# Set steps for the loads of states and decay sums, and a state-space visit spread over three steps, in a one-core decoder layer

## The chip, the cores and the metric

The kernel runs on one core of one Trainium2 chip. The metric is the device time of one execution in microseconds (us). The kernel before has a median of 1779.08 us over three runs (1777.47 to 1779.08).

## The reference

One inference step of a decoder layer for 256 prompt tokens and 64 sample tokens (8 sequences of 8), 320 tokens together, in fp32. One input projection makes the columns of two head groups; a gated MLP and a state-space mixer (SSD) work on them; an output projection adds both up; a convolutional FFN follows.

```python
x = x + RMSNorm_post( W_out [ chunkMLP(h) || SSD(h) ] ),   h = RMSNorm_pre(x)
x = x + RMSNorm_post( ConvFFN(RMSNorm_pre(x)) )
# SSD, per head:
h_t = exp(dt_t a) h_{t-1} + dt_t x_t B_t^T,  y_t = h_t C_t
```

The SSD has 32 heads in 4 groups of 8. The prompt is computed in two chunks of 128 tokens as products with decay matrices. The 8 sample sequences each start from a stored state (64 x 128 per head) that the kernel must read, decay, add to and write back: per group 8 loads and 8 stores of 128 x 512 values.

## The kernel before

**Products.** Each fp32 weight is split into a rounded high part and the remainder, each activation likewise, and three matmuls give one fp32 product (`accumulate`, lines 151 to 156). Weights come in slabs of 512 KB (`slab`, line 110): SyncE loads `wraw` (three buffers), ScalarE casts it to `whi` (line 124), VectorE subtracts to get `wlo` (line 125); both also have three buffers. A slab is 24 matmuls of 128 x 128 by 320. `project` (line 189) runs 8 slabs into four PSUM banks of the pool `mm`, one per 128 columns, and hands each bank to an eviction function; `chunk_out` (line 248) multiplies 512 rows of the output weight in 16 column blocks through the same four banks and adds each block into an accumulator on VectorE (line 261). A second pool, `ms`, has four banks for everything else.

**Order of the work.** SyncE, ScalarE and VectorE take their instructions in the order in which a scheduler puts them when the program is built. Inside the state-space part the stages come in a row by hand (lines 1121 to 1137): X1 (the x columns of group 1), chunk 3, z0 (the z columns of group 0, `heads_out`), X2, chunk 4, z1, X3, chunk 5, z2, z3, chunk 6, chunk 7, and then the FFN. The X projections evict through `conv_proj` (lines 467 to 480): two multiplies into `pad`, one ScalarE and three VectorE steps of the convolution `cv` (line 474), then SiLU. The z projections evict through `scaled` (line 405).

The state-space work of a group runs between these matmuls. `ssd(g)` (line 855) is a generator; a list `bg` holds the generators, and `tick` (line 175) is called after each slab (line 211) and after two column blocks of a chunk. It runs the next step of the first generator once as many matmuls have been issued as that step asked for at its last `yield`; `advance` (line 166) keeps these due counts. Each group has these steps:

- visit 0 (lines 861 to 934): loads six state tiles `st` (three pairs; `load_state`, line 868) and the fourth pair into two buffers of the tag `cs`; copies x of the samples fourfold (`x4`); transposes x; makes `cb` and `cms`. It ends with `yield 120 if g == 0 else 48`.
- the big visit (lines 936 to 998): transposes of the samples' x (`x_of_samples`), the prompt's first chunk state `s1`, the products of C with all four state pairs (`with_c`, line 948), for group 0 the casts of b (`b_of_samples`, lines 837 to 842, which read `b4`), both splits of x (`samples_split`, lines 901 to 908: `xq`, `xsp` and the multiplies into `xdt`), the multiplies of `yo_to_xdt` (line 978), and the decay of the fourth pair on GpSimd (`shrunk`, line 959).
- 13 steps (lines 1046 to 1064): `end(i)` adds the new part to a state pair and stores it from ScalarE's queue; `shrunk` decays a pair; `decays` (line 1006) makes decay factors for a head, and for every second head loads the sums it needs (`load_sums`, line 875) into a `cs` buffer at that moment and exponentiates a part of them (`cpx`, line 1012); `products(j)` (line 1025) multiplies for two heads.
- `final`, which adds and stores the prompt's state.

The z projections are called with `quiet=4`: no step runs after their last slabs. At the end of a z projection, `z_evac` runs any steps still missing.

Of the kernel before, what the change touches and what calls it, by code (L numbers as in the profile page):

```python
# [9 lines left out]
F32 = mybir.dt.float32  # L10
# [3 lines left out]
ALU = mybir.AluOpType  # L14
# [20 lines left out]
def hybrid_step(  # L35
# [115 lines left out]
    def accumulate(ps, w, xhi, xlo, first, last):  # L151
        whi, wlo = w
        made_so_far[0] += 3
        pe.matmul(ps, whi, xhi, start=first, stop=False)  # L154
        pe.matmul(ps, whi, xlo, start=False, stop=False)  # L155
        return pe.matmul(ps, wlo, xhi, start=False, stop=last).ins  # L156

# [5 lines left out]

    bg, side, due, made_so_far = [], [], {}, [0]

    def advance(tasks, task):

        try:
            due[task] = made_so_far[0] + (next(task) or 0)
            return True  # L170
        except StopIteration:
            tasks.remove(task)
            return False

    def tick():
        for task in list(side):
            if made_so_far[0] >= due.get(task, 0):
                advance(side, task)
        while bg and made_so_far[0] >= due.get(bg[0], 0):
            if advance(bg, bg[0]):  # L180
                return
# [7 lines left out]
    def project(w, c0, evac, width=512, spare=False, late=None, quiet=0, ready=None, after=None, ahead=1, rate=1, more=None, held=None):  # L189
# [248 lines left out]
    def in_order(ap):  # L438

        return ap.rearrange("p (i j f) -> p j i f", j=4, f=32)  # L440
# [6 lines left out]
    with ExitStack() as mctx:  # L447
# [374 lines left out]
        with tc.tile_pool(name="sd", bufs=1) as sd:  # L822
# [7 lines left out]
            for c in range(2):  # L830
                act.copy(btok[:, c].rearrange("p (j i f) -> p j i f", j=4, f=32), in_order(b_raw[:, 512 * c:512 * c + 512]))
            b4 = sd.tile([P, 2, 512], F32, tag="xsp", name="b4", bufs=1)
            for i in range(2):
                o = NP + 32 * i
                sp.dma_start(b4[:, i], b_d[o:o + 32].unsqueeze(0).broadcast_to([4, 32, 512]))

            def b_of_samples():
                for i in range(2):
                    act.copy(bsp[:, i].rearrange("p (j i f) -> p j i f", j=4, f=32), in_order(b4[:, i]))
                    for rs in (slice(32, 64), slice(96, P)):  # L840
                        h = bsp[rs, i].rearrange("p (j i f) -> p j i f", j=4, f=32)
                        dve.tensor_tensor(out=h, in0=in_order(b4[rs, i]), in1=h.bitcast(F32), op=ALU.subtract)

# [11 lines left out]
            def ssd(g):  # L855
# [4 lines left out]

                def load_state(i):

                    if i < 3:
                        st = [sd.tile([P, 512], F32, tag="st", name="st", bufs=6) for _ in range(2)]
                    else:
                        st = [sd.tile([P, 2, NT], F32, tag="cs", name="st3", bufs=3).rearrange("p i n -> p (i n)")[:, :512] for _ in range(2)]
                    for h in range(2):
                        sp.dma_start(st[h], state_ssm[4 * h + i, g])
                    return st

                def load_sums(j):
# [23 lines left out]
                def x_of_samples(i):  # L895
                    ps = misc("xt_ps")
                    for j in range(4):
                        by_token(ps[:, P * j:P * j + P], rows[i][:, P * j:P * j + P], 0)
                    return ps

                def samples_split(i, ps):
                    xq = sd.tile([P, 512], F32, tag="xde", name="xq", bufs=2)
                    times(xq, ps, 3 + i)
                    act.copy(xsp[:, i], xq)
                    dve.tensor_tensor(out=xsp[64:, i], in0=xq[64:], in1=xsp[64:, i].bitcast(F32), op=ALU.subtract)
                    for r in range(2):
                        at = slice(64 - 64 * r + 32 * i, 96 - 64 * r + 32 * i)
                        times(xdt[at, 2, 256 * r:256 * r + 256], ps[at, 256 * r:256 * r + 256], 2, at, slice(4 * r, 4 * r + 4))

                for c in range(2):  # L910
# [4 lines left out]
                    if c == 0:  # L915
                        x0d = decayed(0, 0)
                rows.append(fourfold(sd.tile([P, 4, P], F32, tag="xde", name="x4", bufs=2), xs, 1).rearrange("p k n -> p (k n)"))
                ps = misc("cb_ps")
# [20 lines left out]
                s1 = sd.tile([P, 512], F32, tag="s1", name="s1", bufs=1)  # L939

                ps_yo = misc("yo_ps")

                def with_c(i, st):

                    for r in range(2):
                        for h in range(2):
                            row = 64 * r + 32 * h
                            pe.matmul(ps_yo[row:row + 32, :256], cms[:, 4 * h + i, :], st[h][:, 256 * r:256 * r + 256],
                                      start=i == 0, stop=i == 3, tile_position=(0, row))

# [37 lines left out]
                for i in range(4):  # L988
                    with_c(i, sts[i])
# [35 lines left out]
                def products(j):  # L1025
# [9 lines left out]
                    def hs(hl):  # L1035
# [9 lines left out]
                                             op0=ALU.mult, op1=ALU.add)  # L1045
                ends = {2: 3, 4: 0, 6: 1, 9: 2}
                heads = {0: 0, 1: 1, 3: 2, 4: 3, 5: 4, 7: 5, 8: 6, 10: 7}
                for n in range(13):
                    if n == 0:
                        for i in (3, 0):  # L1050
                            bms[i] = picked(i)
                    if n in ends and not (n == 9 and g == 3):
                        end(ends[n])
                    if n in (2, 4):
                        bms[n // 2] = picked(n // 2)
                    if n in (1, 3, 5):
                        shrunk(n // 2, sts[n // 2])
                    if n in heads:
                        decays(heads[n])
                    if n in (7, 12):  # L1060
                        products(0 if n == 7 else 2)
                        products(1 if n == 7 else 3)
                    if n < 12:
                        yield 24

# [11 lines left out]
                if g == 3:  # L1077
                    rest.extend([lambda: end(2, pool), final()])
                else:
                    yield 24  # L1080
                    for _ in final():
                        pass
# [4 lines left out]
            def heads_out(g):  # L1087
# [4 lines left out]
                def z_evac(j, ps):  # L1092
# [3 lines left out]
                    with first():  # L1096
                        scaled(ps, AF.Silu, zs)
                        dve.tensor_tensor(out=y[:, j, :], in0=y[:, j, :], in1=zs, op=ALU.mult)
                        add_square(ssq, y[:, j, :], j == 0, dve)
                project(w_in, Z0 + 512 * g, z_evac, quiet=4)  # L1100

                def norm():
                    yield 24
                    small = partial_sums(ssq, ssq_d[g])
                    yield 24
                    rb = tp.tile([P, NT], F32, tag="pv", name="rb", bufs=4)
# [369 lines left out]
```

## Time and profile before

| | |
|---|---|
| median of 3 runs | 1779.08 us |
| profiled execution | 1780.13 us |
| its span (first to last instruction) | 1778.3 us |
| granted TensorE clock, mean | 0.998 |
| TensorE busy | 1762.1 us (99%) |
| VectorE busy | 1179.3 us (66%) |
| ScalarE busy | 827.1 us (47%) |
| GpSimd busy | 288.6 us (16%) |
| HBM read and written | 274.21 MB, 15.50 MB |

The profile comes from one execution of the program. PE is TensorE, PEld its weight loads, DVE VectorE, ACT ScalarE, POOL GpSimd, SP SyncE. L125 is line 125 of the kernel. Busy time is that of instructions that compute or copy; what an engine waited for is inferred from semaphore events, and the name behind an arrow is the one that came last. The clock is what the throttle granted to TensorE, 1.00 being full speed.

### The profile page before, as it was taken

Reading aid. Unit: us, or ns where it says so; the run is one execution under the profiler, and the core shown is the slowest. Engines: PE = TensorE matmul, PEld = TensorE weight load, DVE = VectorE, ACT = ScalarE, POOL = GpSimd, SP = SyncE. Lnnn points to the kernel's source line nnn. Section 1 sums busy time; section 2 is a strip of 40 time slices with the busy share of each in tenths; the row PEclk is TensorE's granted clock in tenths of the full one; section 3 lists DMA queues with packets and bytes.
Section 4 is the critical chain, followed back from the end, with each engine's and each line's share of the span. In section 5 each row is a group of like instructions: output and inputs, shape, how many; then the busy total and the mean of one; then the engine's idle time right before and its main releaser. Section 6 shows DMA issues by size and latency. Waiting matters only on the chain.

```text
span 1778.3 us, 30601 instructions
## 1 busy us (share of the span) xinstructions
PE 1762.1 (99%) x11881; PEld 1713.0 (96%) x11881; DVE 1179.3 (66%) x2020; ACT 827.1 (47%) x1199; POOL 288.6 (16%) x624
## 2 busy tenths in 40 slices
PE   9999999999999999999999999999999999999998
PEld 7789999999999989999999999999999999999998
DVE  7549764656868688887865475656656565656575
ACT  5434554333555656655645334343434343433445
POOL 1202220000303131303121011110102010101004
PEclk9999999999999999999999999999999999999999
DMA  7556654555574757655554455454454544554542
GB/s 258 162 151 174 192 169 149 155 154 148 176 237 137 241 163 225 191 156 169 167 159 154 149 152 155 146 157 147 152 154 149 151 152 149 157 151 148 155 150 103
DMA packets 218362, 291.73 MB, mean 164 GB/s; under 512 B 19624, under 2 KB 146984, under 8 KB 218024
## 3 DMA queue, kind: packets, MB, share of 16 engines
q1 hardware_dynamic: 205688, 269.37, 50.2%
q10 hardware_dynamic: 10016, 14.16, 2.2%
q0 software_dynamic: 2512, 6.23, 1.2%
q8 instruction: 94, 1.54, 0.4%
q14 instruction: 52, 0.43, 0.1%
HBM read 274.21 MB, written 15.50 MB: 163 GB/s over the span
## 4 chain that ended last, share of the span: by engine, by line
PE 90%; DVE 5%; DMA 3%; ACT 1%; issue 1%; SPq 0%; ACTq 0%; DVEq 0%
PE ps L154 18%; PE ps L156 18%; PE ps L155 18%; PE pd L155 9%; PE pd L156 9%; PE pd L154 9%; PE ps_v L144 7%; DVE wlo L125 2%; DMA cs<-dacs_d 1%; DMA out_ssm_state_sample<-st 1%; ACT whi L124 1%; PE y_ps L1033 1%; DMA st<-in_state_ssm 0%; PE sg L780 0%; DMA small<-ssq_d 0%
## 5 line engine op out<-in xcount | busy, mean ns | idle before, releaser
L125 DVE TENSOR_TENSOR wlo<-wraw,whi 128x1024 fp32r<-128x1024 f32 (+1 forms) x476 | 582.6, 1225 | 429.8 <-ACT whi L124 427.6
L124 ACT CAST whi<-wraw 128x1024 fp32r<-128x1024 f32 (+1 forms) x475 | 494.7, 1042 | 691.7 <-PE ps L155 363.1
L154 PE MATMUL ps<-h_hi,whi 128*128 128x320 f32 x2268 | 704.2, 311 | 4.5 <-ACT whi L124 2.3
L156 PE MATMUL ps<-h_hi,wlo 128*128 128x320 f32 x2268 | 701.9, 310 | 2.0 <-DVE wlo L125 2.0
L155 PE MATMUL ps<-h_lo,whi 128*128 128x320 f32 x2268 | 701.9, 310 | 0.0
L154 PEld LDWEIGHTS ps<-h_hi,whi 128*128 128x128 f32 x2268 | 426.1, 188 | 8.4 <-ACT whi L124 2.8
L156 PEld LDWEIGHTS ps<-h_hi,wlo 128*128 128x128 f32 x2268 | 426.0, 188 | 2.9 <-DVE wlo L125 2.8
L155 PEld LDWEIGHTS ps<-h_lo,whi 128*128 128x128 f32 x2268 | 426.3, 188 | 0.4
L156 PE MATMUL pd<-fhi,wlo 128*128 128x320 f32 x704 | 218.2, 310 | 0.0
L154 PE MATMUL pd<-fhi,whi 128*128 128x320 f32 x704 | 218.2, 310 | 0.0
L155 PE MATMUL pd<-flo,whi 128*128 128x320 f32 x704 | 218.2, 310 | 0.0
L154 PE MATMUL pd<-ohi,whi 128*128 128x320 f32 x448 | 138.6, 309 | 0.1
L156 PE MATMUL pd<-ohi,wlo 128*128 128x320 f32 x448 | 138.2, 309 | 0.0
L155 PE MATMUL pd<-olo,whi 128*128 128x320 f32 x448 | 138.1, 308 | 0.0
L154 PEld LDWEIGHTS pd<-fhi,whi 128*128 128x128 f32 x704 | 132.1, 188 | 0.0
L155 PEld LDWEIGHTS pd<-flo,whi 128*128 128x128 f32 x704 | 132.1, 188 | 0.0
L156 PEld LDWEIGHTS pd<-fhi,wlo 128*128 128x128 f32 x704 | 132.1, 188 | 0.0
L1241 POOL COPY ptf<-pad 128x2 f32<-128x2 f32 x88 | 21.2, 240 | 602.7 <-DVE pad L1229 602.0
L261 DVE TENSOR_TENSOR acc_ffn<-acc_ffn,pd 128x320 f32<-128x320 f32 (+1 forms) x161 | 77.5, 482 | 37.8 <-PE pd L156 36.3
L154 PEld LDWEIGHTS pd<-ohi,whi 128*128 128x128 f32 x448 | 84.1, 188 | 1.3 <-issue 0.9
L155 PEld LDWEIGHTS pd<-olo,whi 128*128 128x128 f32 x448 | 84.1, 188 | 0.3
L156 PEld LDWEIGHTS pd<-ohi,wlo 128*128 128x128 f32 x448 | 84.1, 188 | 0.1
(333 smaller groups left out, 1890.0 us busy)
## 6 DMA issues: line engine op xcount, KB each, us to landing
wraw<-in_ffn_w_up SPq DMA_DIRECT2D x176, 512.0 KB, 3.7
wraw<-in_w_in SPq DMA_DIRECT2D x140, 512.0 KB, 3.8
wraw<-in_ffn_w_down SPq DMA_DIRECT2D x88, 512.0 KB, 3.4
wraw<-in_w_out SPq DMA_DIRECT2D x64, 512.0 KB, 3.5
st<-in_state_ssm SPq DMA_DIRECT2D x32, 256.0 KB, 4.4
out_ssm_state_sample<-st ACTq DMA_DIRECT2D x30, 256.0 KB, 3.6
cs<-dacs_d SPq DMA_DIRECT2D x16, 320.0 KB, 4.8
xr<-in_xT SPq DMA_DIRECT2D x4, 640.0 KB, 4.5
```

Of the source, the lines that this page charges most:

```text
L124: rounded[:] = [act.copy(hi, raw).ins]
L125: dve.tensor_tensor(out=lo, in0=raw, in1=hi.bitcast(F32), op=ALU.subtract)
L144: made = pe.matmul(out, xi, w[g][wi], start=first and begins, stop=last and ends)
L154: pe.matmul(ps, whi, xhi, start=first, stop=False)
L155: pe.matmul(ps, whi, xlo, start=False, stop=False)
L156: return pe.matmul(ps, wlo, xhi, start=False, stop=last).ins
L261: added_last[:] = [dve.tensor_tensor(out=acc[:, nb, ts], in0=acc[:, nb, ts], in1=ps[:, ts], op=ALU.add).ins]
L1033: pe.matmul(ps[64 * i:64 * i + 64, cols], w(hl), x(hl, m, cpx), tile_position=(0, 64 * i), **flags)
L1241: pool.tensor_copy(ptf[:, k, :], pad[:, 256:258])
```

## The change

The generators now yield two numbers: the matmuls until the next step is due, and the least room it wants. `tick` is told how many matmuls the projection still has for its open banks, and runs a step only if that is enough; a chunk always has room (10000). The z projections lose `quiet=4`. A variable `last_made` keeps the last matmul of `accumulate`, so that loads can be put behind it in the order (`tc.issue_after`; this orders the program and adds no semaphore of TensorE to the loads).

For each group:

- state pairs of the next group are loaded at steps 7, 9 and 12 of this one (group 0's are loaded in its visit 0); the fourth pair is loaded into `cs` buffers (`st3`) in visit 0 for the products with C alone, and loaded again into `st` buffers at step 4, to be decayed, added to and stored;
- sums are loaded in visit 0 (pair 0), at step 0 (pairs 1 and 2) and at step 7, or 6 for the last group (pair 3);
- the big visit stops after the first split of x; the second split is step 0, the multiplies into `xdt` and `yo_to_xdt` are step 1. Group 0's big visit is due after 96 matmuls and not 120, which puts it behind the fifth of X1's eight slabs in the built order, and not into chunk 3; group 1's visit 0 goes from behind z0 to two slabs before z0's end;
- group 0's copies of b are loaded after the fourth pair and the first sums, into buffers of `s1` and `xde` and not that of `xsp`, and `b_of_samples` is ordered behind the last product with C;
- state ends run in the order 0, 1, 2, 3 (before 3, 0, 1, 2), and the last group has one step less.

Cut to its core:

```diff
-    def tick():
+    def tick(room=10000):
+        def may(task):
+            at, least = due.get(task, (0, 0))
+            return made_so_far[0] >= at and room >= least
...
-                    tick()
+                    tick(3 * nb * (KD - k0 - nk) if nb == len(js) else 24 if js[0] == 0 else 0)
...
-            b4 = sd.tile([P, 2, 512], F32, tag="xsp", name="b4", bufs=1)
-            for i in range(2):
-                o = NP + 32 * i
-                sp.dma_start(b4[:, i], b_d[o:o + 32].unsqueeze(0).broadcast_to([4, 32, 512]))
+            b4 = [sd.tile([P, 512], F32, tag=tag, name="b4", bufs=n) for tag, n in (("s1", 1), ("xde", 2))]
...
-                sts = [load_state(i) for i in range(3)]
-                rows = [sd.tile([P, 2, NT], F32, tag="cs", name="x4", bufs=3).rearrange("p i n -> p (i n)")[:, :512]]
-                fourfold(rows[0].rearrange("p (k n) -> p k n", n=P), xs, 0)
-                sts.append(load_state(3))
+                sts = sts_of[g]
+                if g == 0:
+                    sts += [load_state(0, i) for i in range(3)]
+                st3 = [sd.tile([P, 2, NT], F32, tag="cs", name="st3", bufs=3).rearrange("p i n -> p (i n)")[:, :512] for _ in range(2)]
+                for h in range(2):
+                    sp.dma_start(st3[h], state_ssm[4 * h + 3, g])
+                cs_of = {0: load_sums(0)}
+                if g == 0:
+                    for i in range(2):
+                        o = NP + 32 * i
+                        sp.dma_start(b4[i], b_d[o:o + 32].unsqueeze(0).broadcast_to([4, 32, 512]))
...
-                yield 120 if g == 0 else 48
+                yield 96 if g == 0 else 48, 72
...
                 if g == 0:
-                    b_of_samples()
+                    with tc.issue_after(visited):
+                        b_of_samples()
...
-                for i in range(2):
-                    samples_split(i, ps_x[i])
+                samples_split(0, ps_x[0])
                 act.copy(s1, ps_s)
-                yo_to_xdt()
-                shrunk(3, sts[3])
-                yield 24
+                yield 24, 0
...
-                        cs = load_sums(j)
+                        cs = cs_of[j]
...
-                ends = {2: 3, 4: 0, 6: 1, 9: 2}
-                heads = {0: 0, 1: 1, 3: 2, 4: 3, 5: 4, 7: 5, 8: 6, 10: 7}
-                for n in range(13):
+                ends = {2: 0, 5: 1, 7: 2, 10: 3}
+                picks = {0: (0, 1), 2: (2,), 5: (3,)}
+                shrinks = {0: 0, 3: 1, 5: 2, 8: 3}
+                e = 1 if g == 3 else 0
+                heads = {0: 0, 1: 1, 3: 2, 4: 3, 5: 4, 7: 5, 9 - e: 6, 10 - e: 7}
+                states = {4: (g, 3), 7: (g + 1, 0), 9: (g + 1, 1), 12: (g + 1, 2)}
+                decays_of = {0: (1, 2), 7 - e: (3,)}
+                for n in range(13 - e):
...
+                        samples_split(1, ps_x[1])
+                    if n == 1:
+                        for i in range(2):
+                            samples_rows(i, ps_x[i])
+                        yo_to_xdt()
...
+                    with tc.issue_after(last_made[0]):
+                        for j in decays_of.get(n, ()):
+                            cs_of[j] = load_sums(j)
+                        if n in states and states[n][0] < 4:
+                            sts_of[states[n][0]].append(load_state(*states[n]))
...
-                    if n < 12:
-                        yield 24
+                    if n < 12 - e:
+                        yield 24, 48 if n + 1 in (0, 1, 2, 5, 7, 10) and (g < 3 or n < 7) else 0
...
-                project(w_in, Z0 + 512 * g, z_evac, quiet=4)
+                project(w_in, Z0 + 512 * g, z_evac)
```

More of the change, by code (lines that the diff above doesn't have):

```diff
@@ L1 @@
 from contextlib import ExitStack, contextmanager, nullcontext
-from itertools import repeat
 import concourse.bass as bass
@@ L155, in accumulate @@
         pe.matmul(ps, whi, xlo, start=False, stop=False)
-        return pe.matmul(ps, wlo, xhi, start=False, stop=last).ins
+        last_made[0] = pe.matmul(ps, wlo, xhi, start=False, stop=last).ins
+        return last_made[0]
     def rows_of(w, k0, nk, c0, n):
@@ L831, in hybrid_step, with load_state @@
                 act.copy(btok[:, c].rearrange("p (j i f) -> p j i f", j=4, f=32), in_order(b_raw[:, 512 * c:512 * c + 512]))
-            b4 = sd.tile([P, 2, 512], F32, tag="xsp", name="b4", bufs=1)
-            for i in range(2):
-                o = NP + 32 * i
-                sp.dma_start(b4[:, i], b_d[o:o + 32].unsqueeze(0).broadcast_to([4, 32, 512]))
+            b4 = [sd.tile([P, 512], F32, tag=tag, name="b4", bufs=n) for tag, n in (("s1", 1), ("xde", 2))]
             def b_of_samples():
                 for i in range(2):
-                    act.copy(bsp[:, i].rearrange("p (j i f) -> p j i f", j=4, f=32), in_order(b4[:, i]))
+                    act.copy(bsp[:, i].rearrange("p (j i f) -> p j i f", j=4, f=32), in_order(b4[i]))
                     for rs in (slice(32, 64), slice(96, P)):
                         h = bsp[rs, i].rearrange("p (j i f) -> p j i f", j=4, f=32)
-                        dve.tensor_tensor(out=h, in0=in_order(b4[rs, i]), in1=h.bitcast(F32), op=ALU.subtract)
+                        dve.tensor_tensor(out=h, in0=in_order(b4[i][rs]), in1=h.bitcast(F32), op=ALU.subtract)
+            def load_state(g, i):
+                st = [sd.tile([P, 512], F32, tag="st", name="st", bufs=6) for _ in range(2)]
+                for h in range(2):
+                    sp.dma_start(st[h], state_ssm[4 * h + i, g])
+                return st
+            sts_of = {g: [] for g in range(4)}
             def by_head(ap):
@@ L897, in x_of_samples @@
                     for j in range(4):
-                        by_token(ps[:, P * j:P * j + P], rows[i][:, P * j:P * j + P], 0)
+                        by_token(ps[:, P * j:P * j + P], x4[:, i, P * j:P * j + P], 0)
                     return ps
@@ new lines, in ssd @@
+                picks = {0: (0, 1), 2: (2,), 5: (3,)}
[5 more added lines that the diff above has]
+                for n in range(13 - e):
+                    if n == 0:
+                        samples_split(1, ps_x[1])
+                    if n == 1:
+                        for i in range(2):
+                            samples_rows(i, ps_x[i])
+                        yo_to_xdt()
+                    if n in ends and not (n == 10 and g == 3):
+                        end(ends[n])
+                    for i in picks.get(n, ()):
+                        bms[i] = picked(i)
+                    if n in (6, 12 - e):
+                        products(0 if n == 6 else 2)
+                        products(1 if n == 6 else 3)
+                    with tc.issue_after(last_made[0]):
[3 more added lines that the diff above has]
+                            sts_of[states[n][0]].append(load_state(*states[n]))
+                    if n in shrinks:
+                        shrunk(shrinks[n], sts[shrinks[n]])
@@ L1077, in ssd @@
                 if g == 3:
-                    rest.extend([lambda: end(2, pool), final()])
+                    rest.extend([lambda: end(3, pool), final()])
                 else:
-                    yield 24
+                    yield 24, 24
                     for _ in final():
```

45 lines of the change are left out of this document (16 added, 29 removed).

## The prediction

> **What bounds the kernel now.** I read the page's first part, then the busy time by stretches of time, then the waits of each engine in the stretch that the change touches, and last the chain of waits around each stall.
>
> ```profile
> span 1778.3 us, 30601 instructions
> PE 1762.1 (99%) x11881; PEld 1713.0 (96%) x11881; DVE 1179.3 (66%) x2020; ACT 827.1 (47%) x1199; POOL 288.6 (16%) x624
> ```
> ```profile
> 420.00:835.00 415.00, 405.39 (x2925) 386.97 (x2924) 325.16 (x567) 235.79 (x413) 102.48 (x116) 1.00 0.60 185
> ```
>
> TensorE bounds the kernel: 1778.3 - 1762.1 = 16.2 us of idle time in all. The second fence is one row of the table by stretches (start:end, length, busy PE, PEld, DVE, ACT, POOL, granted clock, DMA share, GB/s). From 420 to 835 us the four groups' state-space work runs between projections, and 415.00 - 405.39 = 9.61 of the 16.2 us are lost there. The diff touches nothing outside, and TensorE does the same products after it: only this idle time, and clock lost with it, can be won. Where it lies:
>
> ```profile
> 438.00:448.00 10.00, 7.47 (x40) 6.94 (x40) 5.05 (x5) 4.36 (x6) 0.00 (x0) 0.83 0.67 191
> 474.00:479.00 5.00, 4.58 (x29) 3.99 (x28) 4.88 (x8) 4.97 (x10) 4.36 (x7) 1.00 0.33 105
> 508.00:514.00 6.00, 4.83 (x32) 4.31 (x31) 2.68 (x5) 4.94 (x12) 0.74 (x1) 1.00 0.44 144
> 554.00:559.00 5.00, 4.38 (x30) 4.12 (x30) 4.90 (x14) 0.38 (x1) 1.03 (x1) 1.00 0.16 46
> 586.00:594.00 8.00, 6.52 (x59) 5.69 (x58) 7.15 (x12) 6.68 (x15) 0.92 (x1) 1.00 0.78 272
> 634.00:642.00 8.00, 5.92 (x39) 5.39 (x38) 8.00 (x11) 5.18 (x11) 4.69 (x4) 1.00 0.13 26
> sum 42.00, PE 33.70 PEld 30.44 DVE 32.65 ACT 26.50 POOL 11.74; mean PE 5.62 PEld 5.07 DVE 5.44 ACT 4.42 POOL 1.96
> ```
> ```profile
> PE ps L154 <- ACT whi L124: 2.3, 2, 1.8
> PE ps L154 <- DVE ev L405: 2.1, 2, 1.2
> PE ps L156 <- DVE wlo L125: 2.0, 3, 0.7
> PE y_ps L1033 <- DVE cs L1022: 1.5, 2, 1.0
> ```
>
> Six stretches of 42.00 us hold 42.00 - 33.70 = 8.30 us of idle time, nearly all of the 9.61. The waits (total, times, longest) say on what: weight halves cast or subtracted late, PSUM banks emptied late, decays late. In the first stretch the clock was also granted at 0.83, so (1 - 0.83) x 10.00 = 1.7 us more went in slower matmuls. So **10.0 us** can be won at most.
>
> The Trainium skill ("TensorE: Matmul & The Clock Gate", Part 1: The HAM clock gate) puts half speed behind an idle window of about 3.4 us. The trace fell to 0.83 with 10.00 - 7.47 = 2.53 us idle. By the page alone the 1.7 us would not be there and the sum below would be 1.7 us less gain; the trace decides.
>
> **The change, part by part.**
>
> *First visit, b's copies.* These are SyncE's, ScalarE's and TensorE's rows (start, duration, idle before):
>
> ```profile
> 429.17 1.25 SPq L835 DMA_DIRECT2D b<-b_d  x2
> 431.28 3.64 SPq L868 DMA_DIRECT2D st<-in_state_ssm  x5
> 443.99 0.38 SPq L118 DMA_DIRECT2D wraw<-in_w_in  x1
> ```
> ```profile
> 435.88 0.62 ACT L839 CAST bsp<-b 128x512 fp32r<-128x512 f32 x1 [4.03 <-DMA b<-b_d]
> 441.14 0.62 ACT L839 CAST bsp<-b 128x512 fp32r<-128x512 f32 x1 [4.12 <-DMA b<-b_d]
> 441.66 1.99 ACT L124 CAST whi<-wraw 128x1024 fp32r<-128x1024 f32 x2
> ```
> ```profile
> 459.13 0.31 PE L156 MATMUL ps<-h_hi,wlo 128*128 128x320 f32 x1
> 462.80 1.03 PE L427 MATMUL xt_ps<-ident,x 128*128 128x128 f32 x8
> 464.63 1.93 PE L948 MATMUL yo_ps<-st,cb_cms 128*32 128x256 f32 x32
> ```
>
> ScalarE takes its instructions in order. The casts of b stood ahead of two weight casts and waited for loads issued at 429 that landed at 435.9 and 441.1; TensorE starved. After the change the copies of b are loaded behind the fourth state pair and cast behind the big visit's state products and one weight slab later. That takes away 2.53 + 1.7 = **4.2 us**.
>
> It also brings work forward. The big visit (transposes, s1, products of C with four state pairs: 462.80 to 464.63 + 1.93, 3.8 us on TensorE) leaves the chunk and goes behind the fifth of X1's eight slabs. Moved, it costs TensorE nothing in itself. A slab is 24 matmuls that start 0.147 us apart, 3.5 us. X1 ended at 459.4, so now at 459.4 - 4.2 + 3.8 = 459.0; three slabs and 3.8 us earlier, at 444.7, the big visit starts. On VectorE, in the built order, these now stand ahead of X1's evictions (the means, ns, are second behind the bar):
>
> ```profile
> L842 DVE TENSOR_TENSOR bsp<-b,bsp 32x512 fp32r<-32x512 f32 x4 | 2.7, 685 | 6.8 <-ACT bsp L839 6.8
> L886 DVE TENSOR_TENSOR xq<-xt_ps,dt 128x512 f32<-128x512 f32 x8 | 5.5, 683 | 0.1
> L1022 DVE TENSOR_TENSOR cs<-cs,cb_cms 128x320 f32<-128x320 f32 x32 | 18.0, 579 | 2.9 <-ACT cs L1020 2.8
> L905 DVE TENSOR_TENSOR xsp<-xq,xsp 64x512 fp32r<-64x512 f32 x8 | 9.2, 1160 | 0.3 <-ACT xsp L904 0.2
> L886 DVE TENSOR_TENSOR xdt<-xt_ps,dt 32x256 f32<-32x256 f32 x16 | 6.7, 420 | 0.4
> L125 DVE TENSOR_TENSOR wlo<-wraw,whi 128x1024 fp32r<-128x1024 f32 x97 | 122.8, 1268 | 39.8 <-ACT whi L124 39.5
> L467 DVE TENSOR_TENSOR pad<-ps,r 128x256 f32<-128x256 f32 x12 | 5.0, 414 | 0.0
> L468 DVE TENSOR_TENSOR pad<-ps,r 128x64 f32<-128x64 f32 x12 | 2.5, 210 | 0.0
> L474 DVE SCALAR_TENSOR_TENSOR cv<-pad,prm,cv 128x344 f32<-128x344 f32 x36 | 22.6, 654 | 1.1 <-ACT cv L472 1.1
> ```
>
> Let the second copy of b land at t. Its cast ends at t + 0.6 (the 0.62 above), two of the four bsp subtracts at t + 2.0, two xq 3.4, one cs 3.9; the xsp subtracts wait for ScalarE's casts of them and end at about 7.5 (an estimate), two xdt 8.3, wlo 9.6, the first bank's two pads 10.2. From there follow two xdt, one yo multiply (taken as 0.42 like xdt), pads, one cv, wlo, pads, three cv, wlo and the fourth bank's pads: 0.84 + 0.42 + 0.62 + 0.65 + 1.27 + 0.62 + 1.96 + 1.27 + 0.62 = 8.3, so t + 18.5. The pool has four banks, so chunk 3's first column block (12 matmuls, 1.76 us) needs bank 0 at 459.0 and its fourth needs bank 3 at 459.0 + 5.3 = 464.3. So nothing is lost while t is below 464.3 - 18.5 = **445.8**, and each us beyond costs one.
>
> When is t? A slab is cast once TensorE has left the slab three before, and its raw buffer is loaded again after its subtract. X1's sixth slab is cast from 444.7 - 7.0 = 437.7, subtracted by 440.0; the load behind it and then b's copies go out at about 440.5. Before, they landed 6.7 us (first) and 11 to 12 us (second) after issue; that gives 447.2 to 452. Less is under way ahead of them now, since the states went out first. I take 448.5: a cost of 2.7; at 452 it is 6.2, at the best nothing. I charge **2.7** (0 to 6.2). The fourth pair's loads go out one slab earlier, at 437; TensorE needs them at 447.9, behind transposes and three pairs, and ScalarE's exponent on the first sums needs its load at about the same time; both are charged nothing, and if that cover is gone they are the third rival.
>
> *Loads at set steps.*
>
> ```profile
> 497.32 6.01 DMA out_ssm_state_sample<-st
> 503.78 5.16 DMA cs<-dacs_d
> 509.03 0.42 ACT cpx L1012
> 510.27 0.94 ACT whi L124
> 511.24 1.24 DVE wlo L125
> ```
> ```profile
> 573.11 3.31 DMA out_ssm_state_sample<-st
> 576.48 4.91 DMA cs<-dacs_d
> ```
>
> This is the chain of waits into two stalls. A state load on SyncE waits for its buffer's store; the sums' load queued behind it goes out late, cpx waits for that at the head of ScalarE, and a weight cast is behind cpx. The stalls are 6.00 - 4.83 = 1.17 and 8.00 - 6.52 = 1.48, **2.65 us**. In the built order each sums' load now stands some slabs ahead of its decays, and pairs are loaded one at a time behind earlier ends, so I take all of it off. The eight more state loads (second loads of the fourth pair, 256 KB each) add 2.1 MB to 415 us at 185 GB/s (77 MB), 3%: nothing, as the DMA share there is 0.60. What is queued behind a waiting load on SyncE is a weight slab, which SyncE issues about 12 us before its use (443.99, used at 455.9); transfer, cast and subtract take some 6 of these, so a wait of under 6 us costs nothing.
>
> *Room and three steps.* Big-visit work on VectorE stood ahead of evictions at z1's end (634 to 642: VectorE busy 8.00 of 8.00, 2.08 us lost), near z0's end (0.62) and at 474 to 479 (0.42). Steps kept off the ends and spread over three: **3.1 us**. But g1's visit 0 now runs two slabs before z0's end, where it ran after z0. ScalarE has cpx of g1's first sums ahead of a weight cast, which costs only if that load lands over about 3 us behind that visit (I work out 1.5 to 2.5). I charge 0.7, by the nearest row (0.62 at that end before), bounds 0 to 3. For the other ends, with g2's and g3's visits moved alike, 0.8, bounds 0 to 3. Three ScalarE table loads fewer: nothing, ScalarE is 57% busy (235.79 of 415).
>
> **Sum**: -4.2 - 2.65 - 3.1 + 2.7 + 0.7 + 0.8 = -5.75, about **-5.7 us**. The profiled execution took 1780.13 us (span 1778.3 and 1.8 around it); so 1774.4, and against the median of 1779.08, **1773.4**.
>
> **The rivals.**
> 1. *Half given back on VectorE.* The moved work meets evictions as at z1's end. t = 452 makes the first charge 6.2, the two others double to 3.0: -10.0 + 9.2 = -0.8, 1778.3. For it: VectorE at 8.00 of 8.00 before an end did cost 2.08. Against: only g0's work depends on a late load. The Trainium skill ("GPSIMD Engine Reference", 1. Specifications) says that GpSimd shares its SBUF interfaces with VectorE and contends with two-input VectorE instructions. The xsp subtract had durations from 683 to 1494 ns:
>
> ```profile
> L905 DVE TENSOR_TENSOR xsp<-xq,xsp x8: 683/1277/1494, 476.5 to 720.3; 64x512 fp32r<-64x512 f32 x8
> ```
> That agrees; the two at their longest would add 2 x (1.494 - 1.160) = 0.7 us to g0's queue.
> 2. *The loads are not really tied.* The set steps are only an order on SyncE's queue; a load behind a state load that waits for a store still waits. Then the 2.65 stay: -3.1, 1776.0. For it: no new semaphore. Against: the sums go out earlier in that order.
> 3. *Slower: the load queue at X1's end.* If the seventh or eighth slab's load is held to 444, as in the row at 443.99, the fourth pair goes out 7 us later (lands after 449, needed at 447.9, some 2.5 us lost with the sums), and b's copies 7 us later (t = 455.5, bank 3 costs 9.7), with the clock down as at 438 to 448 twice (3.4). With the 1.5 for other ends: -10.0 + 2.5 + 9.7 + 3.4 + 1.5 = +7.1, **1786.2**. It decides from X1's fifth slab being subtracted after about 441. For it: nine loads were out at once there before. Against: what held that slab before was the cast of b, which goes.
>
> **How the numbers follow.** Forecast 0.52; all 10.0 won (1769.1) 0.06; rival 1 0.17; rival 2 0.10; rival 3 0.15. A measurement of this kernel tells about 0.2% from no change, 3.6 us. Forecast and full gain are faster: 0.58. Rivals 1 and 2 are within: 0.27. Rival 3: 0.15. The range reaches from all won, 1769, over rivals 1 and 2 to a first charge at its bound together with both others at theirs (6.2 + 3 + 3 = 12.2, +2.2): 1781.3. It leaves out rival 3.
>
> **What would show it.** ScalarE's cast of bsp should no longer stand before a TensorE stall near 441, and the clock be 1.00 there. Where b's second copy lands tells the first charge: 445.8 or less, no wait on pads at chunk 3's start; 448.5, 2.7 us of waits for pads or wlo there. No cpx should wait over 2 us for its sums with a weight cast behind it. VectorE should not be full just before z1's end. Idle time from 420 to 835 should be about 5.5 us, from 9.61. I am wrong if the fourth pair's products wait for their load, or if the idle time only moves to other projections' ends.

## The result, and the profile after

The changed kernel takes 1769.31 us (median of 4 runs, 1768.6 to 1769.71) against 1779.08: 9.8 us less, a ratio of 0.9946 with a 95% interval of 0.9929 to 0.9964. The forecast was 1773.4, the range 1769.0 to 1781.3: the time lies at its lower end, near the case in which everything is won.

The page's first lines, the same row as shown of before, and six stretches, the last four at the same times as of before (start:end, length, busy PE, PEld, DVE, ACT, POOL, granted clock, DMA share, GB/s):

```profile
span 1766.8 us, 30628 instructions
PE 1756.9 (99%) x11881; PEld 1710.5 (97%) x11881; DVE 1173.2 (66%) x2020; ACT 821.8 (47%) x1196; POOL 295.4 (17%) x624
```
```profile
420.00:835.00 415.00, 412.03 (x2996) 397.20 (x2995) 329.48 (x587) 236.58 (x418) 107.92 (x116) 1.00 0.63 195
```
```profile
444.00:452.00 8.00, 8.00 (x73) 6.32 (x72) 4.13 (x3) 2.35 (x5) 6.26 (x6) 1.00 0.78 231
458.00:468.00 10.00, 7.62 (x41) 7.28 (x41) 9.91 (x23) 9.88 (x21) 8.46 (x12) 0.83 0.33 108
508.00:514.00 6.00, 6.00 (x62) 5.74 (x61) 2.04 (x3) 2.09 (x2) 0.11 (x1) 1.00 0.88 289
554.00:559.00 5.00, 5.00 (x36) 5.00 (x35) 4.25 (x9) 2.07 (x3) 2.94 (x2) 1.00 0.70 226
586.00:594.00 8.00, 8.00 (x56) 7.91 (x55) 5.62 (x9) 3.65 (x5) 0.00 (x0) 1.00 0.82 260
634.00:642.00 8.00, 8.00 (x57) 8.00 (x56) 4.63 (x5) 2.10 (x2) 1.69 (x2) 1.00 0.95 254
```

From 420 to 835 us 415.00 - 412.03 = 2.97 us are idle, from 9.61. In the four later stretches TensorE is busy all the time. They hold other work than before, which now stands up to 10 us earlier, so they alone do not show that the stalls are gone. TensorE's waits from 420 to 835 us (total, times, longest) do: one new stall, where X1 ends, 2.38 us idle with the clock at 0.83 from 458 to 468, and only small ones beside it:

```profile
PE pd L153 <- ACT cs L1030: 2.4, 1, 2.4
PE spread L319 <- DVE rs_r L303: 0.4, 1, 0.4
PE ps L207 <- ACT h_hi L419: 0.2, 1, 0.2
```

The name behind the arrow is that of a ScalarE step that ended just before TensorE went on. The bank is read by the pads, the second of which ended at 460.66, and in fourth_once the same wait (2.8 us) is put down to them; I read it as theirs here too. The chain of waits up to it (start, duration, what):

```profile
440.44 12.02 DMA b<-b_d
452.49 0.62 ACT bsp L841
...
455.38 0.80 ACT bm L965 x2
...
457.83 0.94 ACT whi L123
...
460.81 0.38 PE pd L153
```

and in VectorE's order at that place:

```profile
453.14 2.02 DVE L844 TENSOR_TENSOR bsp<-b,bsp 32x512 fp32r<-32x512 f32 x2 [1.17 <-ACT bsp L841]
455.19 1.29 DVE L897 TENSOR_TENSOR xq<-xt_ps,dt 128x512 f32<-128x512 f32 x2
456.40 0.48 DVE L1033 TENSOR_TENSOR cs<-cs,cb_cms 128x320 f32<-128x320 f32 x1
456.91 1.29 DVE L916 TENSOR_TENSOR xsp<-xq,xsp 64x512 fp32r<-64x512 f32 x2
458.22 0.85 DVE L897 TENSOR_TENSOR xdt<-xt_ps,dt 32x256 f32<-32x256 f32 x2
459.00 1.20 DVE L124 TENSOR_TENSOR wlo<-wraw,whi 128x1024 fp32r<-128x1024 f32 x1
460.13 0.41 DVE L472 TENSOR_TENSOR pad<-ps,r 128x256 f32<-128x256 f32 x1
```

This is the order of the prediction's first charge. b's second copy, issued at 440.44, lands at 452.46. The casts and subtracts of the visit stand ahead of the weight halves and of the first bank's pads on ScalarE and VectorE, so the first bank is free at 460.7, 8.2 us after the landing; X1's last matmul ends at 458.4.

Between the same matmuls on both sides of the stretch the profiled executions took 405.90 us (424.81 to 830.71) and 395.47 us (424.44 to 819.91): 10.4 us less. The rest of the spans' difference of 11.5 lies outside: 0.4 ahead of the stretch and 0.7 at the kernel's end.

### The profile page after: what moved, and what is told of

The parts are those of the page before. It is cut to its first block, busy times and chain, and to the rows that moved or that the text cites. A ratio compares the mean times of both kernels' runs of the same rounds, so it can differ in the third digit from the quotient of the medians.

```text
span 1766.8 us, 30628 instructions
## 1 busy us (share of the span) xinstructions
PE 1756.9 (99%) x11881; PEld 1710.5 (97%) x11881; DVE 1173.2 (66%) x2020; ACT 821.8 (47%) x1196; POOL 295.4 (17%) x624
## 4 chain that ended last, share of the span: by engine, by line
PE 97%; DMA 1%; ACT 1%; DVE 1%; issue 0%; SPq 0%; ACTq 0%; DVEq 0%
PE ps L153 19%; PE ps L154 18%; PE ps L155 18%; PE pd L153 10%; PE pd L154 10%; PE pd L155 10%; PE ps_v L143 7%; PE y_ps L1044 1%; DMA b<-b_d 1%; PE sg L785 0%; PE up_ps L977 0%; PE xt_ps L432 0%; PE yo_ps L959 0%; PE x1p L1363 0%; DMA vt<-in_xT 0%; ACT whi L123 0%
```

## The experiments

Times are medians; ratios are against runs of the kernel before on the same chip, with 95% intervals. The changed kernel's interval is 0.9929 to 0.9964, so a kernel within some 3 us of it is hardly told apart by time; there the traces decide. Every kernel computes everything. First, four kernels on the stall that is left and on single edits of the change.

**b_first.** b's loads at the head of the first visit again, casts ordered behind the cast of X1's fifth slab.

```diff
             b4 = [...]
+            for i in range(2):
+                o = NP + 32 * i
+                sp.dma_start(b4[i], b_d[o:o + 32].unsqueeze(0).broadcast_to([4, 32, 512]))
...
-                    with tc.issue_after(visited):
+                    with tc.issue_after(rounded[0]):
                         b_of_samples()
```

> The changed kernel, with the two loads of b's copies put back to the head of the first visit's loads and their casts ordered behind the weight cast of X1's fifth slab. My theory: the one stall left (2.55 us from start to start at 460.81, and 1.7 us of halved clock behind it) hangs on the landing of b's second copy at 452.5. Issued at 429 it lands near 441, the casts end 442, VectorE has bsp, xq, xsp and xdt done before X1 ends, and the stall goes: 4.1 us off 1769.3, so 1765 to 1766. Rival (VectorE too full at X1's end whatever b does): the stall stays over 1.5 us, 1768 to 1770. Rival (b's slow load pushes the states back): the products with the fourth pair wait, 1 to 3 us near 447, 1767 to 1769.

1766.96 us, 0.9935 (0.9921 to 0.9948). ScalarE's cast of the second copy and TensorE's waits of b_first from 420 to 835:

```profile
439.35 0.62 ACT L844 CAST bsp<-b 128x512 fp32r<-128x512 f32 x1 [3.94 <-DMA b<-b_d]
```
```profile
PE yo_ps L958 <- DMA st<-in_state_ssm: 1.2, 1, 1.2
PE ps L153 <- DVE acc_mix L266: 0.5, 1, 0.5
PE spread L319 <- DVE rs_r L303: 0.4, 1, 0.4
```

The stall at X1's end is gone, and the clock with it (1.00 from 458 to 468); so it hung on b's landing, not on VectorE's amount of work, which is the same here. In its place the fourth state pair comes late by 1.2 us (1.6 from start to start): b's loads push the states back. The theory and the second rival both hold, each for its part.

**b_mid.** As b_first, with b's loads behind the six state loads.

> As b_first, but b's loads stand behind the six state loads and ahead of the fourth pair, about 3.5 us earlier than in the changed kernel. By 12 us from issue to landing the second copy lands at 448 to 449. My sum gives bank 0 free at t + 8 as measured (t was 452.5, its pads ended 460.7), so 457 against a need at 458.6: no stall on it; bank 3 at t + 15 = 464 against 464: none or a few tenths. So 1765 to 1766.5 if the landing decides; 1768 to 1770 if VectorE's amount decides.

1768.82 us, 0.9945 (0.9933 to 0.9958). b's second copy lands at 447.2, ten us after issue. TensorE waits 1.7 us in two pieces for the fourth pair, which now went out right behind b, and 0.8 us for the pads. The landing did decide the pads' wait (2.4 to 0.8), but the expected gain was taken by the states.

**fourth_once.** The fourth pair loaded once; its end first, sums at steps 3 and 5.

```diff
+                sts.append(st3)
...
-                ends = {2: 0, 5: 1, 7: 2, 10: 3}
+                ends = {2: 3, 5: 0, 7: 1, 10: 2}
...
-                states = {4: (g, 3), 7: (g + 1, 0), ...
-                decays_of = {0: (1, 2), 7 - e: (3,)}
+                states = {7: (g + 1, 0), ...
+                decays_of = {3: (1,), 5: (2,), 7 - e: (3,)}
```

> The changed kernel with the fourth pair loaded once: it stays in the sums' buffers until its end, which is first again, and the sums of pairs 1 and 2 are loaded at steps 3 and 5. My theory: what took the stalls at 512 and 588 (2.65 us idle, 3.4 from start to start) away is that the sums' buffers are free early, so here they come back: sums land late, cpx holds a weight cast, 2 to 4 us more than 1769.3, so 1771 to 1773.5. Rival (the set steps of the next group's states did it): no change, 1769 to 1770. The eight loads saved should give nothing.

1768.92 us, 0.9947 (0.9934 to 0.9959): no change. My theory fell. The second load of the fourth pair neither gains nor costs, and the sums' buffers it frees are not what ended the stalls at 512 and 588.

**no_room.** The rule of least room off, `quiet=4` back.

```diff
-            return made_so_far[0] >= at and room >= least
+            return made_so_far[0] >= at
...
-                project(w_in, Z0 + 512 * g, z_evac)
+                project(w_in, Z0 + 512 * g, z_evac, quiet=4)
```

> The changed kernel with the rule of least room switched off and quiet=4 back on the z projections; the big visit stays in three steps. My theory: the stalls before z1's end (2.6 us from start to start) and at z0's end (0.9) come back in whole or part: 1770.5 to 1773. Rival (the three steps alone keep VectorE free): 1769 to 1770.

1769.74 us, 0.9950 (0.9937 to 0.9962): no change either; the stalls at 638 (z1's banks) and at 557 do not come back. At X1's end it waits 2.6 and 1.1 us, and the clock does not fall. Nothing that I undid alone brought back any of the four later stalls. So the next four kernels came from both sides: single edits put into the kernel before, and larger parts taken out of the changed one.

**before_b.** The kernel before, with b's casts ordered behind the cast of chunk 3's first slab.

```diff
                 if g == 0:
-                    b_of_samples()
+                    with tc.issue_after(rounded[0]):
+                        b_of_samples()
```

> The kernel before with one edit: the casts of b are ordered behind the weight cast of chunk 3's first slab (its big visit is in chunk 3), loads as before. The term of the prediction by itself: the stall at 442.75 and the halved clock behind it go, 4.2 us by the prediction's pricing, 4.4 from start to start; the other stalls (512, 557, 588, 638) stay. Against 1778 to 1779: 1773.5 to 1775. Rival (casts late hold the pair updates or bank evictions in chunk 3): 1 to 3 us less gain.

1784.41 us, 1.0034 (1.0021 to 1.0046): slower than before. X1 takes 4.4 us less, so the term was there, but chunk 3 then takes 10.5 us longer. TensorE's waits from 420 to 835, and a stretch of chunk 3:

```profile
PE up_ps L965 <- DVE xsp L905: 4.9, 1, 4.9
PE pd L154 <- DVE acc_mix L261: 3.6, 2, 1.9
PE ps L154 <- DVE ev L405: 2.1, 2, 1.3
```
```profile
468.00:490.00 22.00, 13.52 (x74) 12.62 (x73) 19.53 (x29) 11.80 (x22) 6.64 (x10) 0.84 0.42 140
```

VectorE has X1's convolution, the chunk's additions and the whole big visit with b's subtracts at once (19.53 of 22 us busy), and TensorE loses 8.5 us there and the clock besides. The gain of a stall's end was given back where the work behind it met other work.

**before_96.** before_b, and group 0's big visit due after 96 matmuls, so in X1.

```diff
-                yield 120 if g == 0 else 48
+                yield 96 if g == 0 else 48
```

> The kernel before with two edits: group 0's big visit due after 96 matmuls, and the casts of b ordered behind the weight cast of X1's fifth slab; nothing of set steps, room, three steps, order of ends. New theory after fourth_once and no_room, which gave no stall back: the other stalls go because every step of the groups comes one tick earlier, so that visit 0 and the ends fall elsewhere against the projections' ends; then this alone gives most of it, 1766 to 1769. Rival (each stall is taken away by its own edit: loads, room, three steps): the stalls at 512 to 640 stay, 1773 to 1775.

1773.19 us, 0.9969 (0.9959 to 0.9980). The time is the rival's, at its lower edge, but the rival's mechanism fails: the crowd in chunk 3 is gone (11.2 us better than before_b), and so are the stalls at 512, 557 and 638, with none of the edits to loads, room and steps. Waits of 0.8 us for evictions, 0.8 for decays and 0.3 for a weight remainder are left later on, and 1.6 for the fourth pair. Group 1's visit 0 starts its transposes at 517.8 us here, at 518.3 in the changed kernel and at 532.7 in before. So two edits bring 5.2 us, and the earlier places of the visits, and of the steps behind them, take three of the four later stalls away.

**big_in_chunk.** The changed kernel with 120 again.

> The changed kernel with group 0's big visit due after 120 matmuls again, so behind chunk 3's first slab; all else as changed. X1 ends 3.8 us earlier, near 454.7, and b's second copy lands at 452.5 with four subtracts of 0.7 us ahead of the first bank's pads: a stall of 1.5 to 3 us at X1's end stays. If the tick is what removed the other stalls, some of them come back: 1771 to 1775. If the edits to loads and steps did: 1767.5 to 1770.

1772.52 us, 0.9965 (0.9953 to 0.9978). 2.2 us of waits for pads at X1's end and 3.7 in chunk 3 (2.3 for xsp, 1.4 for the chunk's additions); none behind chunk 3. In the built order group 1's visit 0 stands ahead of z0's end here too, since the z projections let steps run there: the rule of room, with quiet=4 gone, does for the later visits what the earlier start does.

**big_whole.** The changed kernel with the big visit in one piece.

```diff
-                samples_split(0, ps_x[0])
-                act.copy(s1, ps_s)
+                for i in range(2):
+                    samples_split(i, ps_x[i])
+                    samples_rows(i, ps_x[i])
+                act.copy(s1, ps_s)
+                yo_to_xdt()
```

> The changed kernel with the big visit in one piece again (both splits, the multiplies into xdt and yo's); the room rule stays. Theory of the prediction: VectorE is full ahead of z1's end again and bank evictions wait, 1 to 3 us: 1770.5 to 1773. If the room and the earlier tick keep it away from the ends: 1769 to 1770, a little less than that at X1's end, where six more multiplies stand ahead of pads.

1771.29 us, 0.9958 (0.9944 to 0.9972). The stretch at X1's end:

```profile
458.00:468.00 10.00, 5.81 (x26) 5.58 (x25) 9.83 (x19) 8.81 (x19) 3.69 (x8) 0.66 0.32 101
```

Most of the loss is there: 4.2 us idle for the pads, from 2.4, and the clock at 0.66. In the profiles X1 and chunk 3 together take 2.2 us longer, chunk 7 0.8. z1's end shows no wait. Spreading the work bought its 2 us at X1's end, not where I had put it; the time alone, whose interval overlaps the changed kernel's, would not show it.

Three of the last four asked what took the later stalls away; the fourth is about the wait that b_first left.

**chunk_no_room.** big_in_chunk and no_room together. The visits then stand as before, with group 1's visit 0 behind z0 and group 2's big visit two slabs ahead of z1's end; the loads, the order of ends and the three steps are the changed ones.

> The changed kernel with three things undone at once: group 0's big visit due after 120 matmuls, no rule of least room, quiet=4 on the z projections. The visits then stand where they stood before (group 1's visit 0 behind z0, group 2's big visit two slabs ahead of z1's end); set loads, second load of the fourth pair, three steps and order of ends stay. If the places of the visits made the stalls at 557 and 638: they come back, 2 to 3.5 us on top of big_in_chunk's 1772.5, 1774 to 1776. If the three steps and the loads are enough wherever the visits stand: 1772 to 1773.5.

1781.48 us, 1.0017 (1.0008 to 1.0026): the whole gain is lost, 12 us, and more than I expected of either theory. TensorE's waits, and the end of X3 with the start of chunk 5 (at 662.8):

```profile
PE pd L153 <- DVE pad L473: 2.5, 2, 2.3
PE up_ps L977 <- DVE xsp L916: 2.4, 1, 2.4
PE pd L153 <- ACT ohi L419: 1.7, 1, 1.7
PE ps L153 <- DVE acc_mix L266: 1.7, 2, 1.2
PE pd L154 <- DVE olo L420: 0.9, 2, 0.6
```
```profile
660.00:670.00 10.00, 7.27 (x42) 5.93 (x41) 10.00 (x22) 5.17 (x8) 3.93 (x6) 1.00 0.37 124
```

VectorE is full there (10.00 of 10), and the normed heads for chunk 5 (ohi, olo) come late. Some 3 us of the 12 are big_in_chunk's, at X1's end and in chunk 3; the other 9 appear only with both undone. Few stalls are where they were. Apart from the wait for xsp, which is the big visit's own, the larger waits lie within 7 us behind the end of a projection or a chunk, where its banks or the normed heads are wanted. That state-space work in the same places is what delays these is argued from VectorE's rows.

**chunk_both.** The same, and the fourth pair loaded once.

> As chunk_no_room, and the fourth pair loaded once as in fourth_once. If the load edits only matter where the steps stand late, the stalls at 512 and 588 come back here and not in fourth_once: 1 to 3 us above chunk_no_room. If the set loads and ends are not what took these away, no difference within 1 us.

1782.59 us, 1.0022 (1.0012 to 1.0033): 1.1 us over chunk_no_room, at the edge of what can be told. The waits on decays do come back here (4.2 us in two pieces), some others are smaller. So loading the pair twice may help where the steps stand late; where they stand early it does nothing.

**steps_96.** before_96 with the big visit in three steps, loads and ends as before.

> The kernel before_96 (before, group 0's big visit after 96 matmuls, casts of b ordered late, b loaded first) with the big visit's work over three steps as in the changed kernel; loads, sums, order of ends, quiet=4 as before. It stands between before_96 (1773.2) and b_first (1767.0), which has the same early visit and the same loads of b. If the three steps make that difference: 1767 to 1769, and the waits on bank evictions at 731 and on weight remainders at 626 go. If the loads of states and sums and the order of ends make it: 1771 to 1773, and the wait at 579 on decays stays.

1775.66 us, 0.9988 (0.9979 to 0.9997). Not better than before_96 but 2.5 us slower. The longest wait is the one on decays, 2.2 us up to 582:

```profile
PE y_ps L1034 <- DVE cs L1023: 2.7, 2, 2.2
PE yo_ps L950 <- DMA st<-in_state_ssm: 1.6, 1, 1.6
```

Early visits and three steps without the change's loads and order of ends leave it 8.7 us behind b_first, whose visit and b's loads stand alike. It also lacks the rule of room and has quiet=4; no_room shows only that these are not needed beside the changed loads. One thing that differs is how long SyncE's loads wait for stores (total, times, longest), in the order before, steps_96, after, fourth_once:

```profile
SPq L868 <- DMA out_ssm_state_sample<-st: 28.4, 16, 5.6
SPq L875 <- DMA out_ssm_state_sample<-st: 6.9, 6, 3.1
```
```profile
SPq L868 <- DMA out_ssm_state_sample<-st: 22.1, 14, 5.4
SPq L875 <- DMA out_ssm_state_sample<-st: 3.6, 3, 2.6
```
```profile
SPq L850 <- DMA out_ssm_state_sample<-st: 11.7, 20, 2.3
```
```profile
SPq L850 <- DMA out_ssm_state_sample<-st: 6.6, 12, 1.0
SPq L876 <- DMA out_ssm_state_sample<-st: 1.9, 4, 1.1
```

35.3 and 25.7 us against 11.7 and 8.5. The steps of loads and ends, common to the last two, cut these waits. But the waits for stores do not explain the wait at 582. Their totals do not follow the waits on decays: before_96 has 30.6 us and 0.8 us of waits on decays, chunk_no_room 19.6 and none, chunk_both 19.8 and 4.2. And the chain up to 582 in steps_96 holds no store and no load of sums, only VectorE's own queue (X2's convolution, the chunk's additions, a state end, weight remainders):

```profile
574.91 0.97 DVE cv L474 x2
575.89 0.40 DVE acc_mix L261
576.28 1.20 DVE st L969 x2
577.48 1.14 DVE wlo L125
...
580.39 1.14 DVE wlo L125
581.52 0.41 DVE cs L1023
```

So the set loads, the order of ends and the room together are worth the 8.7 us; which of them moves the decays away from that queue stays open.

**b_first_c3.** b_first, and group 0's product of C with the fourth pair moved to step 0.

```diff
-                for i in range(4):
-                    visited = with_c(i, sts[i] if i < 3 else st3)
+                for i in range(3 if g == 0 else 4):
+                    with_c(i, sts[i] if i < 3 else st3)
...
                     if n == 0:
+                        if g == 0:
+                            with_c(3, st3)
                         samples_split(1, ps_x[1])
```

> As b_first, and group 0's product of C with the fourth pair moved from the big visit to the step after it (step 0, in chunk 3). In b_first TensorE waited 1.56 us for that pair's load at 448.9. Theory: the wait goes and nothing takes its place but up to 0.5 us for the first bank's pads at X1's end: 1765.3 to 1766.3 against b_first's 1767.0. Rival (the later product is in the way of chunk 3): no gain, 1766.5 to 1768.

1766.49 us, 0.9934 (0.9921 to 0.9946). The wait for the pair is gone; 0.5 us for pads and 1.1 us for a chunk's additions (at 692) stand in its place. It is not told apart from b_first; both are 2.3 to 2.8 us below the changed kernel's median and are the fastest kernels here, though their intervals overlap the changed kernel's.

## Why the prediction came out as it did

- **What can be won, "10.0 us at most": too small.** I took it from busy time. Matmuls start 0.147 us apart and are shown 0.31 long, so a stall of 1.83 us idle is 1.99 from start to start; 17 stalls of before against 3 make some 2 us that busy time hides. I also left out waits at 495 to 497 and at 797 us. From start to start the stalls that went had cost 11.7 us, with the clock 13.4.
- **First visit, "4.2 us" off: right in size, and not a gain by itself.** The stall went. before_b shows that without the earlier visit it costs 6 us and does not bring 4; with it (before_96) the two bring 5.2.
- **"I take 448.5: a cost of 2.7": the order was right, the term mis-sized.** t was 452.5, the upper end that I had from before's loads (11 to 12 us; 12.0 measured), and I let fewer loads ahead of b shorten it. From t to the first bank's pads 8.2 us passed where I had summed 10.2, since the xsp subtracts ended 1.3 us behind cs and not 3.6. I had let the fourth bank decide, at t + 18.5; its pads ended at 467.6, t + 15.1, and TensorE waited for the first bank alone. The wait was 2.4 us, and the halved clock behind it, which I charged only in the third rival, 1.7: 4.1 against 2.7. The visit as a whole gained next to nothing.
- **"Loads at set steps", 2.65 off: gone, but my chain is not shown to be the reason.** The one at 512 goes with the earlier visit alone (before_96, loads as before). The waits on decays near 580 go only with the group of set loads, order of ends and room (b_first against steps_96), and in steps_96 they come from VectorE's queue and not from a late load of sums. The second load of the fourth pair was no part of it (fourth_once).
- **"Room and three steps", 3.1 off: the stalls went, the causes were others.** I also misread two of the three places. The stall at 557 was not near z0's end, which was at 528, but inside X2, and TensorE waited for a weight remainder; at 474 to 479 it waited for xsp itself and not for an eviction. Only the one at 638 was for z's banks. Neither the room (no_room) nor the three steps (big_whole) is needed for it; what is needed is that the visits stand where they do, which the visit in X1 (before_96 has it alone) and the rule of room (big_in_chunk) each bring about for the later groups. Without both, 12 us are lost.
- **"0.7" and "0.8" for other ends: nothing was lost there.** VectorE was nearly full at these ends all the same: 7.74 of 8 us at z0's (522 to 530) and 7.09 of 8 at z1's (622 to 630). So a full VectorE at an end, which I named as a sign of being wrong, did not by itself make TensorE wait.

By medians forecast and result lie 4.1 us apart; in the profiles the stretch gained 10.4 us where the sum had 5.75. Of these 4.7, 1.5 are charges that did not come and 3.4 stalls that I priced too low (13.4 against 10.0), less the 1.4 by which the first visit cost more; the remaining 1.2 stand in no stall that I can name. That the time still lies in the range is partly luck: the lower end stood for the case in which everything is won, and 4.1 us of that were not. Rival 1's mechanism was real, at X1's end alone. Rival 2's was there (state loads still wait 11.7 us for stores) and cost TensorE nothing. Rival 3 did not occur: the fourth pair was there in time.

The Trainium skill's rule ("TensorE: Matmul & The Clock Gate", Part 1: The HAM clock gate), half speed behind an idle window of about 3.4 us, does not settle it alone. The clock fell behind 2.38 us of idle time in the changed kernel; it did not in no_room, whose waits there were 2.6 and 1.1 us. Its remark there that the window runs freely fits both, and the traces show such a window: within each run the granted clock changes only at whole multiples of 3.413 us (in before_b it falls at 479.65 and at 643.49 us, 48 of them apart). Cut by these windows, the changed kernel and then no_room:

```profile
458.73:462.14 3.41, 1.33 (x9) 1.36 (x10) 3.35 (x8) 3.41 (x10) 2.34 (x4) 1.00 0.21 66
462.14:465.55 3.41, 3.41 (x15) 3.41 (x14) 3.41 (x9) 3.39 (x8) 2.97 (x3) 0.50 0.35 108
```
```profile
456.09:459.51 3.42, 2.20 (x16) 1.94 (x14) 2.91 (x7) 3.42 (x9) 1.66 (x2) 1.00 0.02 6
459.51:462.92 3.41, 2.00 (x13) 2.02 (x14) 3.35 (x9) 3.41 (x10) 2.09 (x4) 1.00 0.42 129
```

The changed kernel's wait puts 2.1 us of idle time into one window, and the next is at half speed; no_room's longer wait is split into 1.2 and 1.4, and nothing follows. So the 1.7 us hang on where a wait lies against these windows, which no edit here sets: that much is chance.

## What to carry to other kernels

Where background work is slotted between matmuls, its place against the ends of the projections can decide more than its amount: undo a step's early start and its guard together before you call either useless, since each can stand in for the other. Price a stall from start to start of the matmuls, with the clock that may fall behind it. And before you end a wait, see which work it has been holding back, and what that will meet.

## What the runs showed of the hardware

The second of the two loads of b, each reading 32 rows four times into 256 KB, landed 10 to 12 us after issue wherever it stood (447.2 after 437.2 in b_mid, 452.5 after 440.4 in the changed kernel), the first 6 to 9, where a state load of the same size has a median of 4.3 us. Loads behind them on SyncE's queue were as slow: a weight slab issued at 442.8 landed at 453.6. Moving a slow load on that queue moves its delay on to the next ones. In the kernel before, from 441 to 444 us, when the loads behind b's copies were still outstanding, the 16 DMA engines' mean busy share was 0.26, about four engines' worth. No run tested why these loads are slow.

A clock that fell was granted again after one window of 3.413 us in both kernels (1.7 us lost), and in big_whole, with 4.2 us idle, after two (0.66 over 10 us). From 420 to 835 us the fourteen traces show nine falls, each behind a window with 1.8 to 2.9 us of idle TensorE. Windows with up to 1.7 us were not followed by one; of three between 1.76 and 1.80, one was. At the kernel's end it fell behind less (0.4 us in before_96), so idle time is not the whole rule.
